# Two layers of a hybrid diffusion step: each large product as one plain fp32 matmul instead of three fp32r ones

## The chip, the cores and the metric

The kernel runs on one core of one Trainium2 chip. The metric is the device time of one execution in microseconds (us); smaller is better. Everything is fp32 in memory. fp32r is a second type on the same 32 bits, to which the kernel rounds operands of TensorE.

## The reference

Two layers, each a SwiGLU half step, a token mixing and a second SwiGLU half step, for 384 tokens: 256 latent tokens (two blocks of 128) and 128 context tokens (the third block).

```python
def swiglu(h, wg, wu, wd):
    return (jax.nn.silu(h @ wg) * (h @ wu)) @ wd
...
    m = jax.nn.silu(cond) @ p["w_ada"][l] + p["b_ada"][l]
...
    x = x + 0.5 * post(swiglu(pre(x, 0), p["ffn1_gate"][l], p["ffn1_up"][l], p["ffn1_down"][l]), 0)
    y, own = token_mix(pre(x, 1), l, p, angles, ctx_kv)
    x = x + post(y, 1)
    x = x + 0.5 * post(swiglu(pre(x, 2), p["ffn2_gate"][l], p["ffn2_up"][l], p["ffn2_down"][l]), 2)
```

`pre` is an RMS norm with scale and shift, `post` one with a gate; scale, shift and gate come from m. `token_mix` makes one input projection, gives its columns to a gated convolution (A), a differential attention (B), a convolution module (C) and a grouped-query attention (D), and makes one output projection. D_MODEL is 1024, the inner width 2816.

## The kernel before

**Tokens and products.** All 384 tokens stay on the chip in x. Before each sub-layer, `pre` norms a block of 128 tokens, turns it on TensorE (`ps_t`, L501) and writes it with scale and shift into h, four tiles of two 128-row chunks each. A large product is then one of three forms: `proj_a` (weights stationary, 384 tokens moving, into `ps_f` for gate and up, into `ps_j` for group A), `proj_b` (tokens stationary, 512 or 256 weight columns moving, into `ps_j` and `ps_gu`), and `rows_out` (tokens stationary, two halves of 512 output columns moving, into `ps_o`: the down and output projections). The small products of the attentions (`ps_s`, `ps_pv`) and the modulation's sums (`ps_first` at L390 for the first norm, `ps_ada` at L291 for all others) are plain fp32 matmuls, the latter in four strips of 32 array columns.

**Three matmuls for one.** Every operand of a large product is kept as a pair: a part rounded to fp32r and the rest. `mm3_a` (L546 to L550), `mm3_b` (L541 to L544) and `rows_out` (L576 to L578) add high x high, high x low and low x high into the same bank:

```python
nc.tensor.matmul(out, lhsT=wh, rhs=hk(h, k, 0, sl), start=start, stop=False)
nc.tensor.matmul(out, lhsT=wh, rhs=hk(h, k, 1, sl), start=False, stop=False)
nc.tensor.matmul(out, lhsT=wl, rhs=hk(h, k, 0, sl), start=False, stop=stop)
```

**The weights' way.** The weights lie in memory in the order of use, 322 blocks of 128 x 1024. `Stream.load` transfers one into one of two stage tiles (`st`, SP's queue); `Stream.pump` splits it into a tile `wu` of a ring of 7: ScalarE casts the high part (L167), VectorE subtracts for the low one (L168). `take(n)` hands over the next n blocks and pumps seven from there on; inside the mix `take(n, False)` pumps only what it hands over, and `tick` one block for each attention unit. `split_pair` (L463) makes the same pair of h, of the hidden rows two at a time in `rows_out`'s `lhs`, and of the mix's four outputs.

**What else runs.** `Ada` sums scale, shift and gate of later norms on VectorE from the ada weights (`ast`, also SP's queue): two steps of 128 x 1024 (L279) for each block, spread over the feed-forward's groups by `more`, with the last sum over rows by TensorE (`ps_ada`, `ps_mod`). The mix's width-31 convolution runs on VectorE (L799). At the end of `rows_out` the last four blocks are done token block by token block, so that `post` and the next `pre` of one block run beside the products of the next. The order on each engine follows from the program's order and the tile scheduler.

Of the kernel before, what the change touches and what calls it, by code (L numbers as in the profile page):

```python
# [13 lines left out]
F32R = mybir.dt.float32r  # L14
# [5 lines left out]
P = 128  # L20
D = 1024
# [11 lines left out]
UNITS = 7  # L33
STAGES = 2
TAIL = 4
MOD_DVE = (2, 0)
# [96 lines left out]
class Stream:  # L133


    def __init__(self, nc, stages, pool):
        self.nc = nc
        self.stages = stages
        self.staged = {}
        self.pool = pool  # L140
        self.units = []
        self.tiles = {}
        self.n_load = 0
        self.n_split = 0
        self.pos = 0
        self.first = 0
# [4 lines left out]
    def load(self, upto):  # L151
        while self.n_load < min(upto, len(self.units)):
            src = self.units[self.n_load]
            n = src.shape[1]
            t = self.stages.tile([P, D], F32, tag="st", name=f"st{self.n_load}")[:, 0:n]
            self.nc.sync.dma_start(out=t, in_=src)
            self.staged[self.n_load] = t
            self.n_load += 1

    def pump(self, upto):  # L160
        nc = self.nc
        while self.n_split < min(upto, len(self.units)):
            i = self.n_split
            self.load(i + 1)
            x = self.staged.pop(i)
            u = self.pool.tile([P, 2, x.shape[1]], F32R, tag="wu", name=f"wu{i}")
            nc.scalar.copy(out=u[:, 0, :], in_=x)  # L167
            nc.vector.tensor_tensor(  # L168
                out=u[:, 1, :], in0=x, in1=u[:, 0, :].bitcast(F32), op=ALU.subtract
            )  # L170
            self.tiles[i] = u
            self.n_split += 1
            self.load(i + 1 + STAGES)
# [13 lines left out]
def kernel(ctx: ExitStack, tc: tile.TileContext, a: dict):  # L187
# [5 lines left out]
    hp = ctx.enter_context(tc.tile_pool(name="hp", bufs=6))  # L193
    sp = ctx.enter_context(tc.tile_pool(name="sp", bufs=STAGES))
# [163 lines left out]
    W = Stream(nc, sp, up)  # L358
# [104 lines left out]
    def split_pair(dst, sl, src):  # L463
        nc.scalar.copy(out=dst[:, 0, :, sl], in_=src)
        nc.vector.tensor_tensor(
            out=dst[:, 1, :, sl], in0=src, in1=dst[:, 0, :, sl].bitcast(F32), op=ALU.subtract
        )

    def new_pairs(s):
        return [hp.tile([P, 2, 2, TOK], F32R, tag="hc", name=nm(s)) for _ in range(4)]  # L470

# [21 lines left out]
    def pre_half(l, i, t, hT, xn, half):  # L493
# [4 lines left out]
        hf = tp.tile([P, 4, P], F32, tag="t2k", name=nm("hf"), bufs=4)  # L498
# [3 lines left out]
        for q in range(4):  # L502
            src = pt[:, q * P : (q + 1) * P]
            sa, sb = A[:, q, cond : cond + 1], B[:, q, cond : cond + 1]
            if q < MOD_DVE[half]:
                nc.vector.tensor_scalar(
                    out=hf[:, q, :], in0=src, scalar1=sa, scalar2=sb, op0=ALU.mult, op1=ALU.add
                )
            else:
                nc.scalar.activation(out=hf[:, q, :], in_=src, func=AF.Identity, scale=sa, bias=sb)  # L510
        for pr in range(2):
            split_pair(hT[2 * half + pr], sl, hf[:, 2 * pr : 2 * pr + 2, :])
# [25 lines left out]
    def hk(h, k, part, sl):  # L538
        return h[k // 2][:, part, k % 2, sl]

    def mm3_b(out, h, k, tsl, wh, wl, start, stop):  # L541
        nc.tensor.matmul(out, lhsT=hk(h, k, 0, tsl), rhs=wh, start=start, stop=False)  # L542
        nc.tensor.matmul(out, lhsT=hk(h, k, 0, tsl), rhs=wl, start=False, stop=False)  # L543
        nc.tensor.matmul(out, lhsT=hk(h, k, 1, tsl), rhs=wh, start=False, stop=stop)  # L544

    def mm3_a(out, h, k, wh, wl, start, stop):  # L546
        sl = slice(0, TOK)
        nc.tensor.matmul(out, lhsT=wh, rhs=hk(h, k, 0, sl), start=start, stop=False)  # L548
        nc.tensor.matmul(out, lhsT=wh, rhs=hk(h, k, 1, sl), start=False, stop=False)  # L549
        nc.tensor.matmul(out, lhsT=wl, rhs=hk(h, k, 0, sl), start=False, stop=stop)  # L550

    def proj_b(out, h, t, units, k0=0, k1=KC):
        tsl = slice(t * P, (t + 1) * P)
        for k in range(k0, k1):
            c = KC // len(units)
            u = units[k // c].rearrange("p s (k n) -> p s k n", k=c)
            mm3_b(out, h, k, tsl, u[:, 0, k % c, :], u[:, 1, k % c, :], k == 0, k == KC - 1)

    def proj_a(out, h, units, cc, k0=0, k1=KC):
        csl = slice(cc * P, (cc + 1) * P)  # L560
        for k in range(k0, k1):
            u = units[k // 4].rearrange("p s (k n) -> p s k n", k=4)
            mm3_a(out, h, k, u[:, 0, k % 4, csl], u[:, 1, k % 4, csl], k == 0, k == KC - 1)

    def rows_out(l, i, lhs, order, nxt):
# [4 lines left out]
        def one(q, u, t, hfs=(0, 1)):  # L570
            pr, s = lhs(order[q])
            for hf in hfs:
# [3 lines left out]
                nc.tensor.matmul(out, lhsT=pr[:, 0, s, tsl], rhs=u[:, 0, hsl], start=(q == 0), stop=False)  # L576
                nc.tensor.matmul(out, lhsT=pr[:, 0, s, tsl], rhs=u[:, 1, hsl], start=False, stop=False)  # L577
                nc.tensor.matmul(  # L578
                    out, lhsT=pr[:, 1, s, tsl], rhs=u[:, 0, hsl], start=False, stop=(q == n - 1)
                )  # L580
# [22 lines left out]
    def ffn(l, i, h, adas, nxt, first=None):  # L603
# [4 lines left out]
        if first is not None:  # L608
            gus = [(bank(nm("ps_gu")), bank(nm("ps_gu"))) for t in range(NT)]
            first(0)  # L610
            for q in range(4):
                us = [u.rearrange("p s (k n) -> p s k n", k=2) for u in W.take(2, q == 3)]
                if q < 2:
                    a0[q + 2] = first_load(q + 2)
                for t in range(NT):
                    if q < 3 and t == FIRST_T:
                        first(q + 1)
                    for j in range(2):
                        for c in range(2):
                            mm3_b(  # L620
# [651 lines left out]
```

## Time and profile before

| | before |
|---|---|
| device time, median of 3 | 1562.38 us (1557.96 to 1562.76) |
| profiled execution, its own time | 1562.17 us |
| its span, first to last instruction | 1560.4 us |
| TensorE matmul, busy | 1500.0 us (96%), 7924 matmuls |
| TensorE weight load, busy | 1319.9 us (85%) |
| VectorE, busy | 1050.7 us (67%) |
| ScalarE, busy | 633.7 us (41%) |
| GpSimd, busy | 126.4 us (8%) |
| granted TensorE clock, mean | 0.986 |
| moved | 260.13 MB, 167 GB/s in the mean |

The engines run side by side, so shares do not add up. Matmuls are pipelined: the rows of two neighbours overlap, and the pace is read from start to start, not from the length of a row. Line numbers are those of the kernel before.

### The profile page before, as it was taken

The numbers are of one execution on the slowest core, as the hardware profiler recorded it, in microseconds if no ns is written. First come the engines' busy times: TensorE is split into PE (matmuls) and PEld (weight loads), VectorE is DVE, ScalarE is ACT, GpSimd is POOL, SyncE is SP. The second block draws the span as 40 slices with busy tenths as digits, with TensorE's granted clock in tenths as the row PEclk, the third lists the DMA queues.
The fourth block names the chain that finished last, engine by engine and source line by source line (L and its number), as shares of the span: only waits on it lengthen the run. The fifth ranks groups of instructions, "written<-read, shape, count | busy, mean of one in ns | idle before, by whom it ended". The sixth has DMA issues, their size and how long they took to land. (4 is left out here: it accounts for less than half of the span.)

```text
span 1560.4 us, 20661 instructions
## 1 busy us (share of the span) xinstructions
PE 1500.0 (96%) x7924; PEld 1319.9 (85%) x7924; DVE 1050.7 (67%) x1454; ACT 633.7 (41%) x1103; POOL 126.4 (8%) x234
## 2 busy tenths in 40 slices
PE   6899999999999999999999999999999999999997
PEld 3699998776887899998879999887768879999885
DVE  3678879867887845677586766984788796333432
ACT  3442233263466632334263333434545764323331
POOL 1101000021001201000021000002100120000000
PEclk9999999998999999999999999999999999999998
DMA  8668767733224555675546656773322245444431
GB/s 307 227 222 261 236 211 236 245 109 98 68 70 145 150 177 179 212 233 172 189 150 215 206 188 200 231 234 110 112 73 92 72 160 175 134 132 138 135 122 41
DMA packets 73619, 260.13 MB, mean 167 GB/s; under 512 B 9728, under 2 KB 9856, under 8 KB 73520
## 3 DMA queue, kind: packets, MB, share of 16 engines
q1 hardware_dynamic: 68112, 246.32, 48.5%
q0 software_dynamic: 4976, 11.70, 2.7%
q8 instruction: 62, 1.02, 0.3%
q10 hardware_dynamic: 432, 0.79, 0.1%
q14 instruction: 37, 0.30, 0.1%
HBM read 256.36 MB, written 2.41 MB: 166 GB/s over the span
## 5 line engine op out<-in xcount | busy, mean ns | idle before, releaser
L168 DVE TENSOR_TENSOR wu<-st,wu 128x1024 fp32r<-128x1024 f32 x322 | 391.6, 1219 | 296.5 <-ACT wu L167 295.9
L167 ACT CAST wu<-st 128x1024 fp32r<-128x1024 f32 x322 | 337.0, 1050 | 585.4 <-DMA st<-ws 253.7
L549 PE MATMUL ps_f<-h,wu 128*128 128x384 f32 x1248 | 418.6, 335 | 0.0
L548 PE MATMUL ps_f<-h,wu 128*128 128x384 f32 x1248 | 418.4, 336 | 0.0
L550 PE MATMUL ps_f<-h,wu 128*128 128x384 f32 x1248 | 418.3, 335 | 0.0
L279 DVE SCALAR_TENSOR_TENSOR acc<-ast,sc,acc 128x1024 f32<-128x1024 f32 x224 | 281.6, 1281 | 27.5 <-DMA ast<-w_ada 26.9
L548 PEld LDWEIGHTS ps_f<-h,wu 128*128 128x128 f32 x1248 | 234.9, 188 | 7.8 <-issue 4.2
L550 PEld LDWEIGHTS ps_f<-h,wu 128*128 128x128 f32 x1248 | 235.0, 188 | 0.0
L549 PEld LDWEIGHTS ps_f<-h,wu 128*128 128x128 f32 x1248 | 235.0, 188 | 0.0
L576 PE MATMUL ps_o<-wu,hid_s 128*128 128x512 f32 x528 | 206.5, 391 | 0.0
L577 PE MATMUL ps_o<-wu,hid_s 128*128 128x512 f32 x528 | 206.0, 390 | 0.0
L578 PE MATMUL ps_o<-wu,hid_s 128*128 128x512 f32 x528 | 205.5, 389 | 0.0
L576 PEld LDWEIGHTS ps_o<-wu,hid_s 128*128 128x128 f32 x528 | 99.1, 188 | 26.1 <-issue 5.9
L578 PEld LDWEIGHTS ps_o<-wu,hid_s 128*128 128x128 f32 x528 | 99.1, 188 | 20.6
L577 PEld LDWEIGHTS ps_o<-wu,hid_s 128*128 128x128 f32 x528 | 99.1, 188 | 20.0
L543 PE MATMUL ps_j<-wu,h 128*128 128x512 f32 (+1 forms) x192 | 73.1, 381 | 5.3 <-DVE wu L168 5.3
L542 PE MATMUL ps_j<-wu,h 128*128 128x512 f32 (+1 forms) x192 | 74.5, 388 | 0.0
L544 PE MATMUL ps_j<-wu,h 128*128 128x512 f32 (+1 forms) x192 | 72.6, 378 | 0.0
L676 ACT ACTIVATE sg<-ps_f 128x384 f32<-128x384 f32 x78 | 38.0, 487 | 83.4 <-PE ps_f L550 79.3
L799 DVE SCALAR_TENSOR_TENSOR cacc<-upad,late,cacc 128x399 f32<-128x399 f32 x120 | 69.9, 630 | 0.0
L337 POOL DMA_DIRECT2D gd<-grow x24 | 11.7, 496 | 676.0 <-DVE grow L329 676.0
L677 DVE TENSOR_TENSOR hid<-sg,ps_f 128x384 f32<-128x384 f32 x78 | 42.9, 549 | 23.3 <-PE ps_f L550 23.3
(234 smaller groups left out, 1701.0 us busy)
## 6 DMA issues: line engine op xcount, KB each, us to landing
st<-ws SPq DMA_DIRECT2D x320, 512.0 KB, 3.9
ast<-w_ada SPq DMA_DIRECT2D x128, 512.0 KB, 4.4
a<-ada SPq DMA_DIRECT2D x16, 512.0 KB, 9.3
G<-gd POOLq DMA_DIRECT2D x12, 512.0 KB, 4.7
brow<-b_ada POOLq DMA_DIRECT2D x24, 64.0 KB, 5.6
prow<-norm_post POOLq DMA_DIRECT2D x24, 64.0 KB, 6.1
x<-x_sample SPq DMA_DIRECT2D x2, 512.0 KB, 5.2
x<-x_prompt SPq DMA_DIRECT2D x1, 512.0 KB, 8.9
```

The costliest lines, as they stand in the source:

```text
L167: nc.scalar.copy(out=u[:, 0, :], in_=x)
L168: nc.vector.tensor_tensor(out=u[:, 1, :], in0=x, in1=u[:, 0, :].bitcast(F32), op=ALU.subtract)
L279: nc.vector.scalar_tensor_tensor(out=self.acc[c], in0=w, scalar=s1, in1=self.acc[c], op0=ALU.mult, op1=ALU.add)
L542: nc.tensor.matmul(out, lhsT=hk(h, k, 0, tsl), rhs=wh, start=start, stop=False)
L543: nc.tensor.matmul(out, lhsT=hk(h, k, 0, tsl), rhs=wl, start=False, stop=False)
L544: nc.tensor.matmul(out, lhsT=hk(h, k, 1, tsl), rhs=wh, start=False, stop=stop)
L548: nc.tensor.matmul(out, lhsT=wh, rhs=hk(h, k, 0, sl), start=start, stop=False)
L549: nc.tensor.matmul(out, lhsT=wh, rhs=hk(h, k, 1, sl), start=False, stop=False)
L550: nc.tensor.matmul(out, lhsT=wl, rhs=hk(h, k, 0, sl), start=False, stop=stop)
L576: nc.tensor.matmul(out, lhsT=pr[:, 0, s, tsl], rhs=u[:, 0, hsl], start=(q == 0), stop=False)
L577: nc.tensor.matmul(out, lhsT=pr[:, 0, s, tsl], rhs=u[:, 1, hsl], start=False, stop=False)
L578: nc.tensor.matmul(out, lhsT=pr[:, 1, s, tsl], rhs=u[:, 0, hsl], start=False, stop=(q == n - 1))
```

## The change

Each large product becomes one matmul of fp32 operands. The pairs, their splits and the stage tiles go. A block of weights is transferred straight into a ring of 17 tiles (4 KB a partition each, where the ring of 7 had 8 KB). `take(n, ahead)` first loads what it hands over, then up to `ahead` blocks more, none beyond 15 from the block in hand. The hidden rows are read where they were written; h and the mix's outputs have one part, in a pool of 10 tiles of half the size. The scale and shift of `pre_half` alternate between VectorE and ScalarE and write h directly.

```diff
-UNITS = 7
-STAGES = 2
+UNITS = 17
+SLACK = 2
 TAIL = 4
-MOD_DVE = (2, 0)
...
     def load(self, upto):
-        while self.n_load < min(upto, len(self.units)):
+        while self.n_load < min(upto, len(self.units), self.first + UNITS):
             src = self.units[self.n_load]
             n = src.shape[1]
-            t = self.stages.tile([P, D], F32, tag="st", name=f"st{self.n_load}")[:, 0:n]
+            t = self.pool.tile([P, D], F32, tag="wu", name=f"wu{self.n_load}")[:, 0:n]
             self.nc.sync.dma_start(out=t, in_=src)
-            self.staged[self.n_load] = t
+            self.tiles[self.n_load] = t
             self.n_load += 1
 
-    def pump(self, upto):
...
-    def tick(self):
-
-        self.pump(min(self.n_split + 1, self.first + UNITS))
-
-    def take(self, n, ahead=True):
-        first = self.first = self.pos
+    def tick(self, n=1):
+
+        self.load(min(self.n_load + n, self.first + UNITS - SLACK))
+
+    def take(self, n, ahead=4):
+        self.first = self.pos
         self.pos += n
-        self.pump(first + UNITS if ahead else self.pos)
-        return [self.tiles.pop(first + j) for j in range(n)]
+        self.load(self.pos)
+        self.load(min(self.n_load + ahead, self.first + UNITS - SLACK))
+        return [self.tiles.pop(self.first + j) for j in range(n)]
...
-    hp = ctx.enter_context(tc.tile_pool(name="hp", bufs=6))
-    sp = ctx.enter_context(tc.tile_pool(name="sp", bufs=STAGES))
+    hp = ctx.enter_context(tc.tile_pool(name="hp", bufs=10))
...
-            if q < MOD_DVE[half]:
+            dst = hT[2 * half + q // 2][:, q % 2, sl]
+            if q % 2:
                 nc.vector.tensor_scalar(
-                    out=hf[:, q, :], in0=src, scalar1=sa, scalar2=sb, op0=ALU.mult, op1=ALU.add
+                    out=dst, in0=src, scalar1=sa, scalar2=sb, op0=ALU.mult, op1=ALU.add
                 )
...
-        for pr in range(2):
-            split_pair(hT[2 * half + pr], sl, hf[:, 2 * pr : 2 * pr + 2, :])
...
     def proj_a(out, h, units, cc, k0=0, k1=KC):
         csl = slice(cc * P, (cc + 1) * P)
         for k in range(k0, k1):
-            u = units[k // 4].rearrange("p s (k n) -> p s k n", k=4)
-            mm3_a(out, h, k, u[:, 0, k % 4, csl], u[:, 1, k % 4, csl], k == 0, k == KC - 1)
+            u = units[k // 4].rearrange("p (k n) -> p k n", k=4)
+            nc.tensor.matmul(
+                out, lhsT=u[:, k % 4, csl], rhs=hk(h, k, slice(0, TOK)), start=(k == 0), stop=(k == KC - 1)
+            )
...
-                nc.tensor.matmul(out, lhsT=pr[:, 0, s, tsl], rhs=u[:, 0, hsl], start=(q == 0), stop=False)
-                nc.tensor.matmul(out, lhsT=pr[:, 0, s, tsl], rhs=u[:, 1, hsl], start=False, stop=False)
-                nc.tensor.matmul(
-                    out, lhsT=pr[:, 1, s, tsl], rhs=u[:, 0, hsl], start=False, stop=(q == n - 1)
-                )
+                nc.tensor.matmul(out, lhsT=pr[:, s, tsl], rhs=u[:, hsl], start=(q == 0), stop=(q == n - 1))
...
-                us = [u.rearrange("p s (k n) -> p s k n", k=2) for u in W.take(2, q == 3)]
+                us = [u.rearrange("p (k n) -> p k n", k=2) for u in W.take(2, 4 if q == 3 else 0)]
...
-                    more(100 if f >= ADA_END else len(fill) / ((ADA_END - f) / 2))
-                    q = hp.tile([P, 2, 2, TOK], F32R, tag="hc", name=nm("hid_s"))
-                    split_pair(q, slice(0, TOK), hid[:, 2 * pr : 2 * pr + 2, :])
-                    cache[pr] = q
-                return cache[pr], f % 2
+                if f == paced[0]:
+                    if f % 2 == 0:
+                        more(100 if f >= ADA_END else len(fill) / ((ADA_END - f) / 2))
+                    paced[0] += 1
+                return hid, f
...
-                    hold["us"] = W.take(4, False)
+                    hold["us"] = W.take(4, 0)
```

`proj_b` and the first product's loop change as `proj_a` does, `first_part` as `pre_half`, and the mix's other outputs as h.

The order on TensorE at the first row chunk of the first down projection (`ps_o` is the output bank, two for each token block, `wu` the block of weights, `hid_s` and `hid` the hidden rows). Before, for the first token block and half of the second:

```order
1053 L576 MATMUL ps_o_1981<-wu_1776,hid_s_2005 128x512
1054 L577 MATMUL ps_o_1981<-wu_1776,hid_s_2005 128x512
1055 L578 MATMUL ps_o_1981<-wu_1776,hid_s_2005 128x512
1056 L576 MATMUL ps_o_1982<-wu_1776,hid_s_2005 128x512
1057 L577 MATMUL ps_o_1982<-wu_1776,hid_s_2005 128x512
1058 L578 MATMUL ps_o_1982<-wu_1776,hid_s_2005 128x512
1059 L576 MATMUL ps_o_1983<-wu_1776,hid_s_2005 128x512
1060 L577 MATMUL ps_o_1983<-wu_1776,hid_s_2005 128x512
1061 L578 MATMUL ps_o_1983<-wu_1776,hid_s_2005 128x512
```

Now, for all three token blocks:

```order
222 L541 MATMUL ps_o_1135<-wu_897,hid_438 128x512
223 L541 MATMUL ps_o_1136<-wu_897,hid_438 128x512
224 L541 MATMUL ps_o_1137<-wu_897,hid_438 128x512
225 L541 MATMUL ps_o_1138<-wu_897,hid_438 128x512
226 L541 MATMUL ps_o_1139<-wu_897,hid_438 128x512
227 L541 MATMUL ps_o_1140<-wu_897,hid_438 128x512
```

One row stands where there were three; the banks' order is the same.

The order on VectorE where the mix of the first layer goes from group D's rows (`dn`, `gqk`) to the first score maximum (`st<-ps_s`), with the split of the q and k weights (`wu<-st`) and the convolution (`cacc`). Before:

```order
339 L820 TENSOR_TENSOR dn_3100<-ps_j_3059,rstd_3098 128x2x2x64
340 L826 TENSOR_TENSOR dn_3100<-ps_j_3059,rstd_3098 128x128
341 L831 TENSOR_TENSOR dn_3100<-dn_3100,gqk 128x256
342 L831 TENSOR_TENSOR dn_3100<-dn_3100,gqk 128x128
343 L168 TENSOR_TENSOR wu_3112<-st_2950,wu_3112 128x1024
344 L168 TENSOR_TENSOR wu_3160<-st_2955,wu_3160 128x1024
345 L872 TENSOR_REDUCE st_3136<-ps_s_3137 128x1
```

Now:

```order
238 L779 TENSOR_TENSOR dn_1747<-ps_j_1722,rstd_1745 128x2x2x64
239 L785 TENSOR_TENSOR dn_1747<-ps_j_1722,rstd_1745 128x128
240 L790 TENSOR_TENSOR dn_1747<-dn_1747,gqk 128x256
241 L790 TENSOR_TENSOR dn_1747<-dn_1747,gqk 128x128
242 L758 SCALAR_TENSOR_TENSOR cacc_1643<-upad_1587,late,cacc_1643 128x399 x5
243 L831 TENSOR_REDUCE st_1770<-ps_s_1771 128x1
```

The two splits are gone, and five steps of the convolution stand in their place.

## Rows read from the trace of the kernel before

**Rows 1.** The page: TensorE's busy time beside the others', and the bandwidth by slice.
```profile
PE 1500.0 (96%) x7924; PEld 1319.9 (85%) x7924; DVE 1050.7 (67%) x1454; ACT 633.7 (41%) x1103; POOL 126.4 (8%) x234
...
DVE  3678879867887845677586766984788796333432
...
GB/s 307 227 222 261 236 211 236 245 109 98 68 70 145 150 177 179 212 233 172 189 150 215 206 188 200 231 234 110 112 73 92 72 160 175 134 132 138 135 122 41
DMA packets 73619, 260.13 MB, mean 167 GB/s; under 512 B 9728, under 2 KB 9856, under 8 KB 73520
```

**Rows 2.** Groups by line and form: xcount | busy us, mean ns of one | idle before.
```profile
L549 PE MATMUL ps_f<-h,wu 128*128 128x384 f32 x1248 | 418.6, 335 | 0.0
...
L576 PE MATMUL ps_o<-wu,hid_s 128*128 128x512 f32 x528 | 206.5, 391 | 0.0
...
L542 PE MATMUL ps_j<-wu,h 128*128 128x512 f32 x144 | 60.4, 420 | 0.0
...
L542 PE MATMUL ps_gu<-wu,h 128*128 128x512 f32 x120 | 48.2, 406 | 0.5 <-ACT h L464 0.5
...
L548 PE MATMUL ps_j<-h,wu 128*128 128x384 f32 x96 | 35.3, 368 | 1.2 <-ACT p L876 1.2
...
L542 PE MATMUL ps_j<-wu,h 128*128 128x256 f32 x48 | 14.1, 294 | 0.0
...
L168 DVE TENSOR_TENSOR wu<-st,wu 128x1024 fp32r<-128x1024 f32 x322 | 391.6, 1219 | 296.5 <-ACT wu L167 295.9
L167 ACT CAST wu<-st 128x1024 fp32r<-128x1024 f32 x322 | 337.0, 1050 | 585.4 <-DMA st<-ws 253.7
```

**Rows 3.** Timeline of TensorE in gate/up and down: start us, length us, instruction.
```profile
129.82 0.33 PE L550 MATMUL ps_f<-h,wu 128*128 128x384 f32 x1
...
139.70 0.33 PE L550 MATMUL ps_f<-h,wu 128*128 128x384 f32 x1
...
284.64 0.39 PE L576 MATMUL ps_o<-wu,hid_s 128*128 128x512 f32 x1
...
299.83 0.39 PE L577 MATMUL ps_o<-wu,hid_s 128*128 128x512 f32 x1
```

**Rows 4.** Plain fp32 matmuls: by tile (ns min/median/max, starts), group, and timeline pieces.
```profile
L871 PE MATMUL ps_s<-kTd,qTd x64: 481/533/585, 423.0 to 1214.0; 32*128 32x384 f32 x64
L871 PE MATMUL ps_s<-kTdp,qTd x32: 270/321/372, 463.9 to 1229.6; 32*128 32x128 f32 x32
L894 PE MATMUL ps_pv<-Vg,wt x96: 217/275/275, 390.4 to 1174.4; 128*128 128x64 f32 x96
L894 PE MATMUL ps_pv<-Vd,wt 128*128 128x64 f32 x96 | 12.9, 270 | 1.2 <-ACT wt L888 1.2
...
38.92 0.40 PE L390 MATMUL ps_first<-a,sc 128*32 128x256 f32 x4
39.78 0.40 PE L390 MATMUL ps_first<-a,sc 128*32 128x256 f32 x4
...
423.02 0.91 PE L871 MATMUL ps_s<-kTd,qTd 32*128 32x384 f32 x2
423.85 0.43 PE L894 MATMUL ps_pv<-Vgp,wt 128*128 128x64 f32 x2
...
439.37 0.88 PE L894 MATMUL ps_pv<-Vd,wt 128*128 128x64 f32 x6 [0.62 <-ACT wt L888]
```

**Rows 5.** Waits of TensorE: us in total, times, longest.
```profile
PE ps_t L501 <- DVE xn L491: 12.1, 15, 1.3
PE ps_j L543 <- DVE wu L168: 5.3, 2, 2.6
PE ps_ht L642 <- DVE sg L639: 4.6, 1, 4.6
```

**Rows 6.** Timeline of ScalarE and VectorE behind the first feed-forward's first product.
```profile
70.02 0.59 ACT L638 ACTIVATE sg<-ps_gu 128x512 f32<-128x512 f32 x1
...
74.82 0.68 DVE L639 TENSOR_TENSOR sg<-sg,ps_gu 128x512 f32<-128x512 f32 x1
```

**Rows 7.** Windows: length, busy us of PE, PEld, DVE, ACT, POOL, granted clock, DMA share, GB/s.
```profile
73.90:80.70 6.80, 5.05 (x18) 5.08 (x19) 5.96 (x10) 3.55 (x5) 0.00 (x0) 0.50 0.66 200
...
377.70:388.00 10.30, 9.70 (x22) 6.43 (x23) 9.97 (x17) 2.77 (x4) 0.33 (x1) 0.50 0.47 150
...
1135.40:1142.30 6.90, 6.73 (x13) 4.14 (x14) 6.90 (x13) 2.76 (x4) 0.00 (x0) 0.51 0.48 161
```

More of the change, by code (lines that the diff above doesn't have):

```diff
@@ L13 @@
 F32 = mybir.dt.float32
-F32R = mybir.dt.float32r
 BF16 = mybir.dt.bfloat16
@@ L461, in rstd_of @@
         return r
[L463 to L467, printed above, removed]
     def new_pairs(s):
-        return [hp.tile([P, 2, 2, TOK], F32R, tag="hc", name=nm(s)) for _ in range(4)]
+        return [hp.tile([P, 2, TOK], F32, tag="hc", name=nm(s)) for _ in range(4)]
     def rstd_two(ss):
@@ L536, in post, with hk @@
             )
[L538 to L550, printed above, removed]
+    def hk(h, k, sl):
+        return h[k // 2][:, k % 2, sl]
     def proj_b(out, h, t, units, k0=0, k1=KC):
@@ L619, in ffn @@
                         for c in range(2):
-                            mm3_b(
-                                gus[t][j], h, 2 * q + c, slice(t * P, (t + 1) * P), us[j][:, 0, c, :],
-                                us[j][:, 1, c, :], q + c == 0, q + c == 4,
+                            nc.tensor.matmul(
+                                gus[t][j], lhsT=hk(h, 2 * q + c, slice(t * P, (t + 1) * P)),
+                                rhs=us[j][:, c, :], start=(q + c == 0), stop=(q + c == 4),
                             )
@@ L1081, in a_fill @@
                     aacc = ac["c"]
+                    if cc == 0:
+                        ac["m"] = hp.tile([P, 2, TOK], F32, tag="hc", name=nm("mTa"))
                     for o, n in SEQS:
@@ L1084, in a_fill @@
                         nc.vector.tensor_tensor(
-                            out=aacc[:, cc, po : po + n], in0=aacc[:, cc, po : po + n],
+                            out=ac["m"][:, cc, o : o + n], in0=aacc[:, cc, po : po + n],
                             in1=ps[:, o : o + n], op=ALU.mult,
                         )
-            def a_split():
-                ac["m"] = mT_a = hp.tile([P, 2, 2, TOK], F32R, tag="hc", name=nm("mTa"))
-                for o, n in SEQS:
-                    po = o + (0 if o == 0 else 1)
-                    split_pair(mT_a, slice(o, o + n), ac["c"][:, :, po : po + n])
             offs = (0, P, 256 + CPAD)
@@ L1173, in mix @@
                     )
-            zS = hp.tile([P, 2, 2, TOK], F32R, tag="hc", name=nm("zS"))
-            split_pair(zS, slice(0, TOK), zT)
-            upw = W.take(1)[0].rearrange("p s (k n) -> p s k n", k=2)
-            mT_c = hp.tile([P, 2, 2, TOK], F32R, tag="hc", name=nm("mTc"))
+            upw = W.take(1)[0].rearrange("p (k n) -> p k n", k=2)
+            mT_c = hp.tile([P, 2, TOK], F32, tag="hc", name=nm("mTc"))
             for oc in range(2):
@@ L1181, in mix @@
                 for k in range(2):
[L1182 to L1187 removed]
+                    nc.tensor.matmul(
+                        ps[:, 0:TOK], lhsT=upw[:, k, osl], rhs=zT[:, k, :], start=(k == 0), stop=(k == 1)
+                    )
+                nc.scalar.copy(out=mT_c[:, oc, :], in_=ps[:, 0:TOK])
             load_gates(l, 1)
```

61 lines of the change are left out of this document (18 added, 43 removed).

## The prediction, made before the changed kernel ran

> **What bounds the kernel now.** I read the page's busy times first. TensorE is busy for 96% of the span, VectorE for 67%, ScalarE for 41% and the transfers run at 167 GB/s on average, against 307 GB/s in the span's best slice [rows 1]. A busy share alone does not say that TensorE works at its own pace, so the second view is the groups of instructions: how many products there are, and of which shapes [rows 2]. The third is the timeline, for the pace. From the row at 129.82 to the one at 139.70 there are 58 rows, 57 steps in 9.88 us: a matmul of 384 columns starts every 173.3 ns, with no hole between them. From 284.64 to 299.83 there are 68 rows: 67 steps of 226.7 ns for 512 columns [rows 3]. With the means of one, 335 and 391 ns [rows 2], 128 columns more cost 56 ns, 0.44 ns each, so 256 columns step by 173.3 - 56 = 117 ns. These steps times the counts below are 3 x (1352 x 0.1733 + 888 x 0.2267 + 48 x 0.117) = 703 + 604 + 17 = 1324 us of the span of 1560.4. The weights' loads run under the matmuls, and nearly all splitting runs beside TensorE: VectorE's 391.6 us on L168 and ScalarE's 337.0 us on L167 [rows 2] reach TensorE in one named wait only, 5.3 us on "wu L168" [rows 5]. So the kernel is bound by the columns that TensorE streams, and the question is what a plain fp32 column costs.
>
> **What a plain fp32 matmul costs.** The counts [rows 2]: 1248 + 96 products of 384 columns and 8 more in ps_w (two layers, two chunks, two k) are 1352; 528 + 144 + 120 of 512 columns and 96 more in the mix's rows_out (two layers, eight chunks, three blocks, two halves) are 888; 48 are of 256. In all 2288 products, three matmuls each. The order of the changed kernel has one MATMUL row where there were three, in the same places. The kernel before already has plain fp32 matmuls: scores, probabilities times values, and the two modulation sums [rows 4]. Two things are read there.
>
> First, the trace keeps two records for one of them: the program has 32 score products of 384 columns in the differential group (two layers, two token blocks, four heads, two maps), the trace 64 rows of "ps_s<-kTd,qTd". Second, a record streams a column at half the pace. The shortest score record takes 270 ns for 128 columns and 481 for 384, so 256 columns more cost 211 ns, 0.82 ns each. Of the split ones a column cost 0.44, about half. The shortest record with a full 128x128 weight is the value product, 217 ns for 64 columns: that is 53 ns under the score record of 128, and 64 x 0.82 = 53, so the full array does not stream faster than the narrow ones [rows 4].
>
> For the step from one record to the next with loads under way, the nearest row is the first modulation's sum: four 32-column strips of the array run side by side, 256 columns each, and the round at 38.92 is followed by the one at 39.78 four rounds later: 216 ns a round, 0.844 ns a column with its overhead [rows 4]. By that, a record of 384, 512, 256 columns costs 324, 432, 216 ns and a product twice that:
> - 384: 0.648 against 3 x 0.1733 = 0.520 us, + 0.128 x 1352 = + 173 us
> - 512: 0.864 against 3 x 0.2267 = 0.680 us, + 0.184 x 888 = + 163 us
> - 256: 0.432 against 3 x 0.117 = 0.351 us, + 0.081 x 48 = + 4 us
>
> Sum: **+340 us**, all on TensorE's path. The bounds: at the bare slope of 0.82 ns a column, products cost 0.630, 0.840, 0.420 us, and the sum is 149 + 142 + 3 = + 294. From above I put 15 ns a record on top of 0.844 ns a column, three times what the split matmuls carry over their columns (173.3 - 384 x 0.4375 = 5): 30 ns more for each of 2288 products, + 68, so + 408. I keep + 340, since its row is a stream of fp32 records in which the next weights are loaded while the last are in use.
>
> A product now needs 2 loads instead of 3. In the value products, six records with a new full weight each take 0.88 us, and a record of this kind takes 270 ns in the mean [rows 4]: they start (0.88 - 0.27) / 5 = 0.12 us apart, more than their 64 columns need. That is the pace of fp32 loads, and 0.12 fits under 0.32. I cost the loads at nothing; the cover is the 324 ns of streaming, and without it the first rival below follows.
>
> **What goes away beside TensorE.** The splits of weights, hidden rows and h leave ScalarE (over 337 us) and VectorE (over 392 us). Neither was the bound, so of this only the waits that stood behind them come back, and the clock that fell after them:
> - "wu L168", 5.3 us [rows 5]: at the mix's start the fourth block of q and k was split only when it was taken (the order on VectorE shows it queued behind d_rows). The ring now holds 15 blocks from the tile in use, and that block is transferred well before. All 5.3 us go.
> - "sg L639", 4.6 us [rows 5]: after ScalarE's 0.59 us on sg, VectorE came to it only at 74.82, behind splits and copies [rows 6]. What stays is sg's own 0.59 + 0.68 us: - 3.3.
> - "xn L491", 12.1 us in 15 waits [rows 5]: between blocks' tails TensorE waits for the norm. The eight tail products that cover one norm grow from 8 x 0.680 = 5.4 to 6.9 us, and ScalarE and VectorE no longer have the two splits of h in this chain. I take half, - 6.
> - The granted clock was 0.5, the lower level of 1.2 GHz, in 73.9 to 80.7, 377.7 to 388.0 and 1135.4 to 1142.3 [rows 7], each time just after one of the first two waits. 24.0 us at half pace cost 12; if the waits go, so do these.
>
> Sum: **- 27 us**. Bounds: nothing, if what comes next in each chain is as late; and 60, if the rest of these waits (1.3 + 6.1 us) goes too and shorter ones give as much as the 27 again. Next late is then the norm's chain itself.
>
> **What else moves.** The ring's transfers go without a stage: each waits for TensorE to have finished a block at least three back. Behind it on SP's queue stand the ada transfers; an ada sum is due one group later, 16 x 0.648 = 10.4 us where it had 16 x 0.520 = 8.3 before, with a free VectorE, so I cost this at nothing. In the first product the blocks of the second quarter are now issued behind four more ada0 transfers: 2 MB, 7 us at 307 GB/s, while the first quarter's twelve products take 12 x 0.864 = 10.4 us. I cost it at nothing, at most 2 us. The 260 MB need 847 us at the best slice's rate, far under the new time.
>
> **Sum:** the profiled execution took 1562.17 us in all (its span is 1560.4), 0.2 us less than the median of three, 1562.38. 1562.2 + 340 - 27 = **1875 us**, 20% slower. From no change a measurement here tells about 0.3%, 5 us.
>
> **Rivals.**
> - *The weight loads are not hidden.* Every weight fills all rows of the array, and a plain fp32 product may have to wait for its loads. For it speaks that a score product alone takes 0.83 us from its start at 423.02 to the next matmul at 423.85 [rows 4], 0.18 over 2 x 0.324. If fp32 products carry that always, 0.18 x 2288 = 412 us come on top of the forecast: 2287 us; if half of it, 2081. It decides if records of 384 columns start over 0.4 us apart. Against it: the split products' 173.3 ns from start to start leave no room for the 168 ns of 384 columns and a load besides [rows 3], and the six value records show one load's pace, not load plus stream. Chance of both 8%. The Trainium skill, "TensorE: Matmul & The Clock Gate", Part 3, says that a load overlaps matmuls in flight only when the row group differs; by that rule this rival would be the forecast, and the trace of the split products disagrees with it.
> - *Faster: the two records of a product overlap.* The narrow shapes might be no measure for a full array with wide columns; if both records ran side by side, as the strips of the modulation do, a product would cost one record, 0.324, 0.432, 0.216 us: - 265 - 220 - 7 = - 492, with the 27 some 1043 us, and VectorE at 1050.7 - 391.6 = 659 us and the transfers at 847 would allow it. The turning point is a product of 0.520 us for 384 columns. Against it: in the lone score product the two records take 0.83 us one after the other, and 217 ns for 64 columns of a full weight fits the slower stream [rows 4]. Chance 3%. The Trainium skill's "Perfetto Trace Analysis", Engine Utilization, halves TensorE's output rate for fp32 low/high in a footnote; read as the rate of a whole product it gives this rival, read as that of one record it is the forecast, and the trace agrees with the second.
> - *More returns than the named waits.* VectorE is at six tenths or more in most slices of the first three quarters [rows 1], so small delays may sit in many places. With + 294 and - 60 the time is 1796. Chance of under 1825: 6%.
>
> **How the numbers follow.** The forecast has 83%, with its bounds 1562 + 294 - 60 = 1796 and 1562 + 408 = 1970; nearer the middle, 1825 to 1930 holds some 8 in 10 of all. Slower by over 0.3%: 96%. Within 0.3%: 1%, out of the last rival, if gains unseen here cancel the cost. Faster: 3%.
>
> **What would show it.** Right: 4576 records at the product lines, two for each product, 324 ns apart in the gate and up projections and 432 in the down projections; no row of the splits; VectorE under 659 us busy and ScalarE under 634 - 337 = 297; "wu" gone from TensorE's waits; TensorE's idle time no larger than before. Wrong: records of one product that start under 260 ns apart at 384 columns (the faster rival), over 400 (bare loads), or holes in TensorE's timeline that end with a transfer of "wu".

## The result, and the profile after

| | before | after |
|---|---|---|
| device time, median of 4 runs each | 1561.96 us (1557.96 to 1562.76) | 1878.18 us (1875.83 to 1881.43) |
| ratio after / before | | 1.2032, 95% interval 1.2002 to 1.2062 |
| profiled execution: own time, span | 1562.17, 1560.4 us | 1876.34, 1874.6 us |

The change makes the kernel 20% slower; the forecast of 1875 us was 3 us off. The page of the changed kernel, beside [rows 1]:

```profile
PE 1820.2 (97%) x5636; PEld 963.6 (51%) x5636; DVE 629.3 (34%) x1024; ACT 247.7 (13%) x629; POOL 118.4 (6%) x234
...
DMA packets 73589, 259.73 MB, mean 139 GB/s; under 512 B 9728, under 2 KB 9856, under 8 KB 73520
```

VectorE lost 421 us of work and ScalarE 386, more than forecast, and none of it is the time of the kernel: TensorE is at 97%. Why it takes longer shows in the groups by line and form on TensorE (count, busy us, mean ns of one, idle before), beside [rows 2]:

```profile
L526 PE MATMUL ps_f<-h,wu 128*128 128x384 f32 x2496 | 809.5, 486 | 0.0
L541 PE MATMUL ps_o<-wu,hid 128*128 128x512 f32 x1056 | 457.5, 593 | 0.0
L518 PE MATMUL ps_j<-wu,h 128*128 128x512 f32 x288 | 132.2, 609 | 0.0
L526 PE MATMUL ps_j<-h,wu 128*128 128x384 f32 x192 | 69.5, 508 | 0.0
...
L518 PE MATMUL ps_j<-wu,h 128*128 128x256 f32 x96 | 22.3, 386 | 0.0
```

Each product has two records: 2496 where [rows 2] has three times 1248. With the rows not shown, the product lines have 4576 records, as forecast. Their pace is read from two pieces of TensorE's timeline, gate and up and then down (start us, length us), beside [rows 3]:

```profile
149.45 5.32 PE L526 MATMUL ps_f<-h,wu 128*128 128x384 f32 x16
...
289.21 5.74 PE L541 MATMUL ps_o<-wu,hid 128*128 128x512 f32 x13
```

Sixteen records span 15 steps and the last one's length: (5.32 - 0.486) / 15 = 0.322 us for 384 columns; (5.74 - 0.593) / 12 = 0.429 us for 512. Over the whole trace the median steps are 323, 429 and 216 ns (256 columns), where the kernel before has 173, 227 and 120.

What TensorE waited for in the changed kernel, all rows (us in total, times, longest), beside [rows 5]:

```profile
PE ps_t L474 <- DVE xn L465: 19.7, 15, 2.6
PE ps_first L370 <- DMA a<-ada: 13.3, 3, 12.9
PE ps_qk L964 <- DVE cacc L758: 4.5, 2, 2.2
PE ps_mo L862 <- DVE mo L953: 2.2, 2, 1.1
PE ps_s L830 <- DVE mTa L1045: 2.0, 2, 1.0
PE ps_mod L380 <- ACT rows L377: 0.5, 1, 0.5
PE ps_gu L581 <- DVE h L1165: 0.4, 1, 0.4
```

"wu" and "sg" are gone, and no transfer of weights is waited for. But the norm's wait grew from 12.1 to 19.7 us, and two waits are new. Between the first 30 us and the last matmul, the low level of the clock, 0.50, is left in four windows (length, busy us of PE, PEld, DVE, ACT, POOL, granted clock, DMA share, GB/s), beside [rows 7]:

```profile
396.60:400.00 3.40, 3.40 (x8) 1.84 (x7) 1.58 (x4) 2.97 (x5) 0.00 (x0) 0.51 0.02 5
492.20:495.60 3.40, 3.40 (x6) 1.89 (x7) 1.53 (x4) 0.70 (x3) 0.00 (x0) 0.50 0.25 102
1314.80:1318.20 3.40, 3.40 (x11) 2.37 (x12) 1.30 (x4) 1.87 (x5) 0.00 (x0) 0.50 0.01 4
1372.80:1376.20 3.40, 3.40 (x5) 1.17 (x4) 3.40 (x8) 1.54 (x5) 0.00 (x0) 0.51 0.00 0
```

That is 13.6 us. Before there were 27.3, with one more stretch of 3.4 us at 425.5 than [rows 7] show. Left out of both counts are the start, where both kernels have a stretch at half pace (in the changed kernel two records of 512 columns start 853 ns apart until 24.5 us; its trace has a record of the clock only from there on), and the end, where TensorE has nothing left to do.

**Where the time went.** The span grew by 314.2 us. Steps times counts give 1323.7 us before and 2704 x 0.323 + 1776 x 0.429 + 96 x 0.216 = 1656 us after: **+332**. The remaining -18 us: the named waits without the first transfer fell from 36.0 to 29.3 us (-6.7), the low clock gave back about half of 13.7 us (-7, an estimate), and some 4 us are not assigned to a row.

### The profile page after: what moved, and what is told of

Same layout as the page of the kernel before. It is cut to its first block, busy times and chain, and to the rows that moved or that the text cites. A ratio compares the mean times of both kernels' runs of the same rounds, so it can differ in the third digit from the quotient of the medians.

```text
span 1874.6 us, 14732 instructions
## 1 busy us (share of the span) xinstructions
PE 1820.2 (97%) x5636; PEld 963.6 (51%) x5636; DVE 629.3 (34%) x1024; ACT 247.7 (13%) x629; POOL 118.4 (6%) x234
## 5 line engine op out<-in xcount | busy, mean ns | idle before, releaser
L526 PE MATMUL ps_f<-h,wu 128*128 128x384 f32 x2496 | 809.5, 486 | 0.0
L526 PEld LDWEIGHTS ps_f<-h,wu 128*128 128x128 f32 x2496 | 472.5, 190 | 332.4 <-DVE hid L638 5.0
L541 PE MATMUL ps_o<-wu,hid 128*128 128x512 f32 x1056 | 457.5, 593 | 0.0
L541 PEld LDWEIGHTS ps_o<-wu,hid 128*128 128x128 f32 x1056 | 199.2, 190 | 249.0 <-issue 246.9
L518 PE MATMUL ps_j<-wu,h 128*128 128x512 f32 (+1 forms) x384 | 154.5, 553 | 0.0
L518 PEld LDWEIGHTS ps_j<-wu,h 128*128 128x128 f32 x384 | 72.4, 194 | 70.1 <-issue 66.4
L526 PE MATMUL ps_j<-h,wu 128*128 128x384 f32 x192 | 69.5, 508 | 0.0
L518 PE MATMUL ps_gu<-wu,h 128*128 128x512 f32 x144 | 62.8, 592 | 0.0
L526 PEld LDWEIGHTS ps_j<-h,wu 128*128 128x128 f32 x192 | 35.5, 194 | 29.9 <-issue 9.1
L581 PE MATMUL ps_gu<-wu,h 128*128 128x512 f32 x96 | 46.6, 620 | 0.4 <-DVE h L1165 0.4
L835 ACT ACTIVATE p<-ps_s,st 128x384 f32<-128x384 f32 (+1 forms) x72 | 36.4, 508 | 62.1 <-DVE st L831 61.8
L518 PEld LDWEIGHTS ps_gu<-wu,h 128*128 128x128 f32 x144 | 27.1, 190 | 33.0 <-issue 33.0
```

What stands on the lines that cost most here:

```text
L518: nc.tensor.matmul(out, lhsT=hk(h, k, tsl), rhs=u[:, k % c, :], start=(k == 0), stop=(k == KC - 1))
L526: nc.tensor.matmul(out, lhsT=u[:, k % 4, csl], rhs=hk(h, k, slice(0, TOK)), start=(k == 0), stop=(k == KC - 1))
L541: nc.tensor.matmul(out, lhsT=pr[:, s, tsl], rhs=u[:, hsl], start=(q == 0), stop=(q == n - 1))
L581: nc.tensor.matmul(gus[t][j], lhsT=hk(h, 2 * q + c, slice(t * P, (t + 1) * P)), rhs=us[j][:, c, :], start=(q + c == 0), stop=(q + c == 4),)
L835: nc.scalar.activation(out=p[:, 0:nk], in_=ps[:, 0:nk], func=AF.Exp, bias=st[:, 0, idx : idx + 1], accum_out=st[:, 1, idx : idx + 1],)
```

## The experiments

Times are medians beside the kernel before in the same batch (1563.17 us for the first four, 1564.85 for the next four, 1566.5 for the last two). Experiments 3, 4 and 10 are a single run each.

**1. The products alone.** In the kernel before, each triple of matmuls becomes one plain fp32 matmul of the high parts; splits, stage tiles and the ring of 7 stay. The same edit is made in `mm3_b` and `rows_out`.

```diff
     def mm3_a(out, h, k, wh, wl, start, stop):
-        nc.tensor.matmul(out, lhsT=wh, rhs=hk(h, k, 0, sl), start=start, stop=False)
-        nc.tensor.matmul(out, lhsT=wh, rhs=hk(h, k, 1, sl), start=False, stop=False)
-        nc.tensor.matmul(out, lhsT=wl, rhs=hk(h, k, 0, sl), start=False, stop=stop)
+        nc.tensor.matmul(out, lhsT=wh.bitcast(F32), rhs=hk(h, k, 0, sl).bitcast(F32), start=start, stop=stop)
```

> The kernel before with its splits, stage tiles and ring of 7, but one plain fp32 matmul of the high parts instead of three fp32r ones; the products with the low parts are left out. Theory (the cost is the columns streamed: two records a product, 323 ns each for 384 columns and 429 for 512): 1352 x (0.646 - 0.520) + 888 x (0.858 - 0.680) + 48 x 0.08 = 170 + 158 + 4 = 332 us more than 1562, less 0 to 20 us of waits that the longer products cover: 1875 to 1895 us, with the same paces as in the changed kernel. Rival (the ring and the unsplit transfers made the difference): under 1700 us, or over 1950.

Measured: 1873.99 us, ratio 1.1993 (1.1974 to 1.2013). Its page:

```profile
PE 1816.5 (97%) x5636; PEld 961.1 (51%) x5636; DVE 1062.7 (57%) x1454; ACT 638.6 (34%) x1103; POOL 127.0 (7%) x234
```

VectorE still does all its splits, 1062.7 us, and the time is that of the changed kernel within their intervals. So the form of the product is the whole slowdown; once it is there, removing the splits and the stages returns nothing that can be measured. This kernel's waits say why, since there was little left to return: behind the first transfer they are 31.3 us in all, and 29.3 in the changed kernel. The largest:

```profile
PE ps_t L501 <- DVE xn L491: 16.0, 15, 2.0
...
PE ps_s L866 <- ACT kTg L847: 7.4, 2, 3.8
PE ps_ht L637 <- DVE sg L634: 1.9, 1, 1.9
```

It has no row of "wu": with the longer products alone, that wait is gone.

**2. The splits' low part alone.** The kernel before without VectorE's subtractions; three fp32r matmuls remain, all of the high parts.

```diff
             nc.scalar.copy(out=u[:, 0, :], in_=x)
-            nc.vector.tensor_tensor(
-                out=u[:, 1, :], in0=x, in1=u[:, 0, :].bitcast(F32), op=ALU.subtract
-            )
...
-        nc.tensor.matmul(out, lhsT=wl, rhs=hk(h, k, 0, sl), start=False, stop=stop)
+        nc.tensor.matmul(out, lhsT=wh, rhs=hk(h, k, 0, sl), start=False, stop=stop)
```

> The kernel before with its three fp32r matmuls, but VectorE's subtractions are gone (weights, h, hidden rows, mix outputs): the high part stands in for the low one, so the corrections of the product are left out. Theory (splits are hidden beside TensorE, only the waits behind them count): the wait on wu (5.3 us), some 2 of 4.6 us on sg, part of 12.1 us on xn and up to 12 us of low clock go, 1540 to 1557 us, the pace of 173 and 227 ns unchanged. Rival (the splits slow TensorE itself, by its reads): steps shorter than 173 ns and a time under 1530 us. Other rival (nothing comes back): 1562 us.

Measured: 1552.05 us, ratio 0.9929 (0.9911 to 0.9947). VectorE falls from 1050.7 to 612.3 us, and 438 us less work buy 11 us. The time is inside the expected range, its parts are not all so: the waits behind the first transfer fell from 36.0 to 27.1 us, but the one on xn grew from 12.1 to 15.5, and the low clock gave nothing back, with five stretches of 27.2 us in all where the kernel before has 27.3. Two of them, at the starts of the mixes (columns as above), and a wait that stands there:

```profile
377.30:384.10 6.80, 6.77 (x21) 5.09 (x22) 5.40 (x12) 2.73 (x8) 0.00 (x0) 0.50 0.01 2
1131.70:1138.50 6.80, 6.80 (x19) 4.81 (x18) 5.11 (x11) 2.23 (x7) 0.00 (x0) 0.50 0.01 2
```

```profile
PE ps_qk L999 <- DVE cacc L793: 3.3, 2, 1.7
```

With the subtractions "wu L168" is gone, a "wu" of 0.8 us on ScalarE's cast is left, and the clock still falls at the start of both mixes. The prediction gave the fall to the wait on "wu". Here a wait of 1.66 us on the convolution (`ps_qk`) ends at 377.3, just where the clock falls: the name of the wait has changed, but a wait is still there.

**3 and 4. Are the weight loads hidden?** In the changed kernel, each product of 384 columns in `proj_a` is cut into pieces of 128 columns, and in a second kernel of 96, with the same weights loaded anew for each piece (shown for 96).

```diff
-            nc.tensor.matmul(
-                out, lhsT=u[:, k % 4, csl], rhs=hk(h, k, slice(0, TOK)), start=(k == 0), stop=(k == KC - 1)
-            )
+            for c0 in range(0, TOK, 96):
+                nc.tensor.matmul(
+                    out[:, c0 : c0 + 96], lhsT=u[:, k % 4, csl], rhs=hk(h, k, slice(c0, c0 + 96)),
+                    start=(k == 0 and c0 == 0), stop=(k == KC - 1 and c0 == TOK - 96),
+                )
```

> The changed kernel with each product of 384 columns in gate, up and group A cut into three of 128, with the same weights: 1344 products, six records each. Theory (weight loads run under the stream, a record takes the longer of its stream, 108 ns, and a load, some 112 ns): six times 0.112 = 0.67 us a product instead of 0.646, + 35 us, 1913 us. Rival (each record of fp32 waits for its load): six times 0.215 = 1.29 us, + 866 us, 2740 us.

> The same with four pieces of 96 columns, eight records a product. Theory (the load's 112 ns is now longer than the 81 ns stream): eight times 0.112 = 0.90 us a product, + 336 us, 2214 us. Rival (loads cost nothing, the stream alone counts): eight times 0.084 = 0.67 us, 1913 us, as with 128 columns.

Measured, a single run each: 1906.83 and 2208.46 us, as this theory had them (1913 and 2214). TensorE's timeline with pieces of 128:

```profile
149.60 2.84 PE L527 MATMUL ps_f<-h,wu 128*128 128x128 f32 x24
```

and with pieces of 96:

```profile
149.66 2.73 PE L527 MATMUL ps_f<-h,wu 128*128 128x96 f32 x23
```

A row here lasts 275 ns in the mean in both, so a step is (2.84 - 0.275) / 23 = 0.112 us for 128 columns and (2.73 - 0.275) / 22 = 0.112 us for 96. A quarter fewer columns save nothing: 0.112 us is a floor for each record. That it is the pace of the loads, and not a fixed cost of a record, fits the value products of the changed kernel, of 64 columns: most of their records start 111 or 112 ns apart, but some 58 or 59 (at 453.04 and 453.10). Under a stream of 323 ns the floor does not show: with bare loads a record of 384 columns would take over 0.4 us. This closes the rival of loads that are not hidden. The Trainium skill's rule in "TensorE: Matmul & The Clock Gate", Part 3, that a load overlaps only where the row group differs, does not hold in these runs: all weights here fill all rows.

**5. The depth of the ring.** The changed kernel with 9 blocks for 17.

```diff
-UNITS = 17
+UNITS = 9
```

> The changed kernel with a ring of 9 blocks instead of 17 (7 ahead of the block in hand instead of 15). Theory (TensorE's stream is the bound and a block is transferred in some 3.6 us while two blocks feed 10 us of products): the same time as the changed kernel, within 0.3%, 1873 to 1884 us. Rival (the deep ring is what keeps TensorE fed): waits of TensorE on transfers of wu, over 1890 us.

Measured: 1883.63 us, ratio 1.2044 (1.2012 to 1.2075), no wait on a weight in its trace. The depth is not needed at this pace; the changed kernel's transfers run at 139 GB/s in the mean, and its best slice has 368.

**6. The norm's wait.** In the changed kernel, the transposes of a token block are written behind the next block's tail products (`turn`).

```diff
+        def turn(t):
+            for half in range(2):
+                pre_half(nxt[0], nxt[1], t, hn, xns_[t], half)
...
         for t in range(NT):
             for hf in range(2):
                 for j in range(TAIL):
                     one(n - TAIL + j, us[j], t, (hf,))
+            if nxt is not None and t > 0:
+                turn(t - 1)
             post(l, i, t, banks[t])
             if nxt is not None:
-                pre(nxt[0], nxt[1], t, hn)
+                xns_[t] = tp.tile([P, D], F32, tag="t4k", name=nm("xn"))
+                pre_norm(t, xns_[t])
+                if t == NT - 1:
+                    turn(t)
```

> The changed kernel, but in the tail of each sub-layer the turning matmuls of a token block's norm are written after the next block's eight products instead of before them; the order on TensorE then has 8 products between a block's last product and its turning, where the changed kernel has 6. Theory (the wait on xn, 19.7 us where half of 12.1 was forecast, comes from the 6 products that cover the norm's chain): two products more, 1.7 us, cover eight waits of 1.03 to 1.08 us in full and 1.7 us of two longer ones: - 12 us, 1866 us. Rival (the wait only moves to the third block): 1878 us.

Measured: 1867.28 us, ratio 1.1947 (1.1923 to 1.1972), under the changed kernel's interval. Its waits:

```profile
PE ps_t L474 <- DVE xn L465: 8.7, 7, 2.2
```

From 19.7 us in 15 waits to 8.7 in 7; the time fell by as much, 11 us by the medians and 13 by the ratios. So the place of the transposes in TensorE's order makes most of that wait. The waits that the expectation puts at 1.03 to 1.08 us are 0.86 to 0.92 in the changed kernel's trace; with them its sum is 8 x 0.9 + 2 x 1.7 = 10.6 us.

**7. The "wu" wait, alone.** In the kernel before, group D of the mix splits one block earlier.

```diff
                 proj_b(ps, h, t, us, 0, 4)
+                if t == 2:
+                    W.pump(W.n_split + 1)
                 run(flush())
```

> The kernel before, but the split of the fourth q and k block is written between the two halves of group D's last projection, ahead of that block's row work, not after it. Theory (the wait on wu at the mix's start made TensorE stand 2.6 us twice, and the clock fell for 10.3 and 6.9 us after it): 5.3 us of wait and 8.6 us of clock go, 1548 us. Rival (the clock falls for another reason): 1557 us. Other rival (the row work that is now later takes the wait's place): 1562 us.

Measured: 1563.04 us, ratio 0.9998 (0.9985 to 1.0011): no change. Its waits:

```profile
PE ps_mod L300 <- ACT rows L297: 5.3, 3, 3.0
...
PE ps_qk L1007 <- ACT kTgp L852: 3.7, 2, 1.8
PE ps_dT L847 <- DVE dr L731: 2.2, 2, 1.4
```

The 5.3 us of "wu" are gone, and the row work behind the moved split comes later by as much: qk and dr take 5.9 us where dr alone took 0.6 before. The low clock also stayed at both mixes, shorter in the first (3.4 us from 389.2) and as long in the second (6.8 us from 1143.6). Here too a wait stands ahead of the fall: the first of `ps_qk`, 1.84 us, ends at 389.1. So a named wait of 5.3 us was worth nothing by itself.

**8 and 9. The two edits together, and a third.** Kernel 8 is the kernel before with the edits of 6 and 7. Kernel 9 adds to 8 that only two blocks, not five, are split ahead behind the first feed-forward's first product:

```diff
-                us = [u.rearrange("p s (k n) -> p s k n", k=2) for u in W.take(2, q == 3)]
+                us = [u.rearrange("p s (k n) -> p s k n", k=2) for u in W.take(2, False)]
...
+            if first is not None:
+                W.pump(W.pos + 2)
```

> The kernel before with both: the early split, and the turning of each norm after the next block's eight products. Theory: two thirds of the 12.1 us on xn go besides, 1540 us. Rival (the chain is hidden as it is, or its wait moves): as with the early split alone. If it is under 1562 by more than 0.3%, it beats both kernels.

> The kernel of the run before with both edits, and a third: behind the first feed-forward's first product only two blocks of weights are split ahead of the hidden rows' first chunk, not five. Theory (the 3.9 to 4.6 us wait on sg comes from splits queued ahead of it on VectorE): some 2.5 us of wait and part of the 3.4 us of low clock behind it go, 1557 us. Rival (the products behind it now wait for their own splits): 1561 us or more.

Measured: 1560.61 us, ratio 0.9977 (0.9963 to 0.9991), and 1560.68 us, ratio 0.9962 (0.9949 to 0.9975). Both missed the gain that was expected of them. The waits of kernel 9:

```profile
PE ps_t L501 <- DVE xn L491: 10.7, 15, 1.3
PE ps_ht L655 <- DVE sg L652: 4.7, 1, 4.7
PE ps_dT L860 <- DVE dr L744: 4.6, 4, 1.5
PE ps_s L886 <- ACT kTg L865: 3.8, 2, 2.0
PE ps_mod L300 <- ACT rows L297: 3.5, 3, 1.5
```

The "sg" wait that the edit was made for stayed at 4.7 us, and deferring the transposes bought 1.4 us of xn here where it bought 11 in the changed kernel. Kernel 9 is still faster than either kernel, by 0.4% than the one before; which of its edits gives that is not settled, and its interval overlaps that of 8.

**10. What bounds the kernel when products are cheap.** The kernel before with one fp32r matmul of the high parts for each product and no subtractions; the same edit is made in `mm3_b` and `rows_out`.

```diff
     def mm3_a(out, h, k, wh, wl, start, stop):
         sl = slice(0, TOK)
-        nc.tensor.matmul(out, lhsT=wh, rhs=hk(h, k, 0, sl), start=start, stop=False)
-        nc.tensor.matmul(out, lhsT=wh, rhs=hk(h, k, 1, sl), start=False, stop=False)
-        nc.tensor.matmul(out, lhsT=wl, rhs=hk(h, k, 0, sl), start=False, stop=stop)
+        nc.tensor.matmul(out, lhsT=wh, rhs=hk(h, k, 0, sl), start=start, stop=stop)
...
```

> The kernel before with one fp32r matmul of the high parts for each product and no subtractions; both products with the low parts are left out. It shows where the kernel stands once a product is cheap. Theory (all other work has the room that it seemed to have): two thirds of 1324 us go, 680 us of TensorE, and the transfers' 260 MB set the end, 847 us at the best slice's rate, 870 to 1000 us. Rival (ScalarE's casts and their waits bind earlier): over 1100 us.

Measured, a single run: 1200.25 us; my range of 870 to 1000 was missed and the rival was right. Its page, and the waits of TensorE, ScalarE and SP:

```profile
PE 816.5 (68%) x3348; PEld 584.5 (49%) x3348; DVE 610.3 (51%) x994; ACT 627.9 (52%) x1103; POOL 127.1 (11%) x234
...
DMA packets 73577, 259.49 MB, mean 217 GB/s; under 512 B 9728, under 2 KB 9856, under 8 KB 73520
```

```profile
PE ps_f L540 <- ACT wu L167: 126.5, 96, 7.2
PE ps_o L566 <- ACT wu L167: 83.7, 61, 3.8
...
ACT wu L167 <- DMA st<-ws: 320.1, 217, 7.8
...
SPq L156 <- ACT wu L167: 518.5, 295, 19.6
```

No engine is over 68%, and TensorE waits 210 us in the first two rows for ScalarE's casts. ScalarE is busy for 52%: its casts wait 320 us for transfers, and the transfers wait 518 us for casts to free one of the two stage tiles. So what binds is this circle through two stages, more than the casts' own time. TensorE's mean granted clock is 0.826. More stages or a direct transfer, which are worth nothing behind plain fp32 products, could have something to return here; that was not run.

## Why the prediction was right, and where two errors met

| term | forecast | measured |
|---|---|---|
| products | +340 | +332: steps 323, 429, 216 ns for 324, 432, 216 |
| "wu" | -5.3 | gone, but +4.5 (cacc) and +2.0 (mTa) new in the mix |
| "sg" | -3.3 | -4.6 |
| "xn" | -6 | +7.6 |
| low clock | -12 | -7 (estimate: half of 27.3 less 13.6 us) |
| beside TensorE in all | -27 | -18 |

**What bounds the kernel: right.** TensorE streams without holes before and after, the loads are hidden (experiments 3 and 4), the second record comes after the first. The two rivals with a time far from the forecast are excluded by the steps: 2 x 0.323 = 0.646 us for a product of 384 columns, neither one record (0.323) nor two with bare loads. Experiment 1 shows that the products alone carry the change, and with it that the third rival, more returns from the splits than the named waits, is out.

**The price of a record: right, 2% high.** It was taken from four strips of the array at 216 ns a round of 256 columns [rows 4]. In the changed kernel 256 columns step by 216 ns, but 384 and 512 by 323 and 429, a little nearer to the bare slope. This is 8 of the 340 us. The upper bound took an overhead of 5 ns for an fp32r matmul; by the steps it is 13 (last section), which leaves the forecast as it was.

**"xn": wrong sign.** The step that failed is "The eight tail products that cover one norm grow from 5.4 to 6.9 us". It counted the products written between two blocks, not those that stand in TensorE's order. In the changed kernel's order the transposes come after six:

```
L541 MATMUL ps_o_1137<-wu_1257,hid_438 128x512
L541 MATMUL ps_o_1138<-wu_1217,hid_438 128x512
L541 MATMUL ps_o_1138<-wu_1233,hid_438 128x512
L474 MATMUL ps_t_1457<-early,xn_1448 128x128 x4
```

Bank 1137 has four and 1138 two; the norm is that of the block before them, and the two norms that follow have six products too: 6 x 2 x 0.429 = 5.1 us. In the order before, at the two tails that lead into a mix, 21 matmuls (7 products, 4.8 us) stood there for the first norm and 38 (8.6 us) for the second; at the other three tails the trace has 24 (5.4 us) and 30 (6.8 us). So the cover of the later norms shrank with the new order, though each product in it is longer. The other half of the term held in part: cover and wait together, the length of the norm's chain, were 4.76 + 1.27 = 6.0 and 8.6 + 1.1 = 9.7 us for the first two norms into a mix, and are 6.0 and 6.1 now. The long chain got shorter, and the cover with it. What the chain takes can be read in the changed kernel's timeline (all engines, rows left out):

```profile
370.79 0.60 ACT L499 ACTIVATE sink<-ps_o 128x512 bf16<-128x512 f32 x1 [2.75 <-PE ps_o L541]
...
375.87 0.75 DVE L465 TENSOR_SCALAR xn<-x,rstd 128x1024 f32<-128x1024 f32 x1 [1.89 <-POOL rstd L453]
...
376.76 1.06 PE L474 MATMUL ps_t<-early,xn 128*128 128x128 f32 x8 [0.87 <-DVE xn L465]
...
385.62 1.07 PE L474 MATMUL ps_t<-early,xn 128*128 128x128 f32 x8 [0.92 <-DVE xn L465]
...
388.50 0.60 ACT L499 ACTIVATE sink<-ps_o 128x512 bf16<-128x512 f32 x1 [0.39 <-PE ps_o L541]
...
389.34 0.54 POOL L667 DMA_DIRECT2D Vg<-cache_gqa_v  x1
389.96 0.30 POOL L449 TENSOR_SCALAR ms<-ss 128x1 f32<-128x1 f32 x1
390.31 0.78 POOL L668 DMA_DIRECT2D kTd<-cache_kT  x1
391.12 0.58 POOL L453 TENSOR_TENSOR rstd<-ms,mhalf 128x1 f32<-128x1 f32 x1
...
395.97 1.33 PE L474 MATMUL ps_t<-early,xn 128*128 128x128 f32 x8 [2.42 <-DVE xn L465]
...
581.07 2.47 DVE L259 SCALAR_TENSOR_TENSOR acc<-ast,sc,acc 128x1024 f32<-128x1024 f32 x2
...
581.60 2.03 POOL L449 TENSOR_SCALAR ms<-ss 128x1 f32<-128x1 f32 x1 [23.70 <-ACT sink L499]
583.46 0.68 DVE L502 TENSOR_TENSOR yg<-ps_o,G 128x512 f32<-128x512 f32 x1
...
584.31 1.42 DVE L506 SCALAR_TENSOR_TENSOR x<-yg,rstd,x 128x512 f32<-128x512 f32 x2 [0.17 <-POOL rstd L453]
...
588.44 1.09 PE L474 MATMUL ps_t<-early,xn 128*128 128x128 f32 x8 [2.52 <-DVE xn L465]
```

From the square at 370.79 to the end of xn at 376.62 are 5.8 us against 5.1 of cover, and TensorE stands for 0.87. Eleven of the 15 waits are of this size, 0.7 to 0.9, and so was the mean before (0.8). The other four carry the growth, 2.4 to 2.6 us each where the longest before was 1.3. Two are the third norm into a mix (395.97): there GpSimd issues cache transfers (389.34, 390.31) between the norm's own small steps, and from 388.50 to the end of xn are 7.3 us. Two are the first norm of an output projection (588.44): there VectorE runs two ada sums (581.07) ahead of the norm's own step `yg`, which it reaches only at 583.46, and `x` starts at 584.31, 3.5 us behind the square of its block (580.81), where the one at 370.79 has 1.8. "ms" on GpSimd, mostly 0.30 us, takes 2.03 and ends with the two sums; but `x` waits for it only 0.17 us longer than VectorE is busy, so the sums ahead of `yg` account for nearly all of the delay without it. Experiment 6 takes 11 us off by moving the transposes back, which shows that the cover sets the wait. What is read of these four delays comes from rows; no run took them away one by one.

**"wu": right on the row, too much on the time.** The wait went, but the order on VectorE had shown what took its place: five convolution steps stand where the two splits were, and `ps_qk` now waits 4.5 us for them. Experiment 7 shows the same in the kernel before: the wait goes, the row work behind it is late instead.

**The clock: half.** The stretch after "sg" (73.9 to 80.7) is gone, those at the mixes' starts are shorter but still there. Experiments 2 and 7 take the "wu" wait away and leave a fall there. That does not refute "if the waits go, so do these", since in neither did the waits go: 1.7 and 1.8 us of `ps_qk` stand ahead of the fall in 2 and 7, and 2.4 us of xn (to 395.97 and 1314.73) ahead of the one in the changed kernel. What failed is that the wait on "wu" would have no successor. A wait is not the whole of it either: the 2.25 us of `ps_qk` that end at 452.2 in the changed kernel have no fall behind them, and its stretch at 492.2 has no wait ahead of it. What starts a fall stays open.

**Beside TensorE in all** the forecast gave back 9 us too much, and the products cost 8 less than forecast. That the two nearly cancel is luck: the 3 us between forecast and median claim more than either part has. The bounds (+294 and -60) held both. What was costed at nothing held: ring, SP's queue, ada and the loads show in no new wait. Not in the forecast was the modulation's wait on "rows" at L300, 4.2 us before, which is gone.

## What to carry to other kernels

Where TensorE streams without holes, a product costs its records times the step of one, and the pace of a form that the kernel already uses in small (here scores and sums in plain fp32) can be read from start to start and carried to the large ones. Work that leaves an engine that was not the bound returns only the waits behind it, and a wait that goes can leave the next in its chain in its place: 438 us less on VectorE were worth 11, and 5.3 us of a named wait nothing. When a cover is counted in instructions, count them in the order that the engine executes, not in the source.

## What the runs showed of the hardware that was not expected

- A plain fp32 record has next to no overhead over its columns: from the timeline, 0.429 - 0.322 = 107 ns for 128 columns more is 0.833 ns a column, 384 of them are 320, and 2 ns of the step are left. An fp32r matmul has more: 226.7 - 173.3 = 53.4 ns for 128 columns, 160 for 384, and 13 ns are left [rows 3]. So three fp32r matmuls cost 0.520 us and two plain records 0.645, 1.24 times as much and not 4/3, as the columns alone would give. The prediction had 0.44 ns a column for fp32r, from the lengths of rows, and so 117 ns for 256 columns where the step is 120.
- The floor of 0.112 us for a record, at 128 as at 96 columns, is 5 ns over the 128-column stream (107 ns by the slope above): from some 134 columns on, by this slope, the loads are hidden (an estimate).
- "ms" on GpSimd took 2.03 us, where it mostly takes 0.30, while VectorE ran two sums of 128 x 1024 without a break, and ended with them (583.63 and 583.54).
- The best slice of the changed kernel moved 368 GB/s, that of experiment 1, with stages, 315, and that of [rows 1] 307. TensorE's first wait did not shrink with it (13.3 us, 12.8 before): it is on the first modulation's own weights.
